# The norm behind the expert stage in place and tile by tile, GpSimd's steps on VectorE, and the order of a feed-forward's first weights

## The chip, the core and the metric

One core of a Trainium2 chip runs the whole program in one launch. Its engines work beside each other, each through its own queue in order: TensorE (PE: matrix products and transposes, with PEld for its weight loads), VectorE (DVE), ScalarE (ACT), GpSimd (POOL), and SyncE (SP), which here issues the DMA transfers. The metric is the device time of one execution in microseconds (us), the median over runs.

## What is computed

256 tokens of 1024 features go through two blocks, one behind the other, all in 32-bit floats.

```python
# block 1, twice (l = 0, 1)
mix = concat(retention, sliding_window, latent_attention)(x @ w_in[l]) @ w_out[l]
x = layer_norm(DEEPNORM_ALPHA * x + mix, ln1_g[l], ln1_b[l])
ffn = grouped_moe(x, router_w, router_bias, exp_w_gate_up[l], exp_w_down[l])
x = layer_norm(DEEPNORM_ALPHA * x + ffn, ln2_g[l], ln2_b[l])
# block 2, twice
h = h + 0.5 * swiglu(rms_norm_2(h, ffn1_norm[l]), ffn1_w1[l], ffn1_w3[l], ffn1_w2[l])
h = h + token_mixer(rms_norm_2(h, mix_norm[l]), w_in[l], ...)
h = h + 0.5 * swiglu(rms_norm_2(h, ffn2_norm[l]), ffn2_w1[l], ffn2_w3[l], ffn2_w2[l])
# at the end
rms_norm_2(h, final_norm)
```

`layer_norm` subtracts the mean over the features, divides by the deviation, multiplies by g and adds b. `rms_norm_2` divides by the root of the mean square and multiplies by a gain. `swiglu(u, w1, w3, w2)` is `(silu(u @ w1) * (u @ w3)) @ w2` with 2816 inner columns. `grouped_moe` has 16 experts, of which each token uses two.

## The kernel before

**Weights.** Every matrix product is made from two halves of each operand: a rounded high half and a low half, the rest. The weights stream in one fixed order from memory through six raw buffers (`raw`, DMA issued by SP); for each piece of up to 1024 columns ACT casts the high half (`whi`, L350) and DVE subtracts to the low one (`wlo`, L351), into five buffers each. A product is then three matmuls (helper `mm`, L411), two with `whi` and one with `wlo`; where the operand's halves lie side by side, the two with `whi` are one matmul of 512 columns (`gemm_halves`).

**Order.** The kernel is written as Python that issues instructions; a scheduler sets each engine's order from that. `tc.issue_after(x)` adds the condition that what follows on the engine of x stands behind x. `tc.manual_schedule(engines=...)` keeps the written order on the engines named (only the changed kernel uses it here).

**The expert stage and its norm.** `moe` ends with 60 filler matmuls (`keep_clock(WARM[2])`, tile `idle`), while DVE adds the stage's sum `ya` to the scaled input (L1197, tile `r`, four steps of 512 columns). `ln_hat` then takes statistics (L570, L571), the inverse root (`rsqrt`, eight small steps for each of the two token tiles of 128, L480 to L489) and writes the normalized `xh`, half by ACT (L583) and half by DVE (L584). Behind layer 0, `affine_T` transposes `xh` on PE (`trx`, L597) and applies g and b to the transposed blocks while it splits them (L605 to L607, tile `x2hl`): that is the input of the next attention, whose first products are `oq` (by `gemm_wide("cq")`) and `okv`. Beside it POOL makes the untransposed input `x` from `xh` and the broadcast rows `gb` (L1528, L1529). Behind layer 1, `xh` is transposed at L1538, DVE applies g and b (L1541, tile `h`, eight blocks), and `take_block` splits each block with the next gain and squares it (`xT_h`, L516, L517, and `sq`, L521).

**A feed-forward** (`ffn`, called four times; the last one has `then=None`) runs over f = 0 to 21, 128 inner columns each: u = x @ w1, v = x @ w3, then the down products f, which stand two steps later. The rms scale is not applied to the input but to u and v. It is computed at f = 0: `rms_columns` adds the squares up on DVE (L526), PE sums over the partitions (`rrow<-cperm,sq`, the column sums), DVE makes the mean (`ms`, L530) and the inverse root (`rsqrt_n`, ten small steps, L462 to L471, last `rs`) and puts it on a diagonal (`dg`, L535); PE turns that into a row (`rrow<-dg`, the row product, `rms_row`), ACT copies it (`row`, L542). Then DVE multiplies u by it (`fhp<-row,fhp`, L1324), ACT takes silu, DVE forms the product with v (L1327 to L1330), and ACT and DVE split it (`fhh`, L1331, L1332). u's low part is brought over by ACT (L1322) and added by DVE (`fhp<-u`, L1323); v's in the same way (`fvl`, L1328, and `fhp<-v`, L1329), and v's bank is free behind that. The last feed-forward also transposes the running state in its second step (`trh`, L1313, copied by ACT to `htok`, L1314).

**Elsewhere**, POOL makes the first product of the rotary step (`rope`, L651, 1024 columns in the attention and 1280 in the mixer), the gated norm weight of the retention (`gg`, L836) and, in the mixer, the sum of a pair of halves (`msum`, L1472, eight each).

## Time and profile before

| | |
|---|---|
| median of three runs | 1735.04 us (1733.93 to 1735.08) |
| profiled execution | 1737.42 us |
| its span | 1735.6 us |
| PE busy | 1673.4 us (96%) |
| DVE busy | 1278.7 us (74%) |
| ACT busy | 988.0 us (57%) |
| POOL busy | 56.2 us (3%) |

The profile is of one execution. Busy times are sums over the instructions of an engine; the idle time of an engine that is not the bottleneck costs nothing. Of interest is where PE idles, what it waits for there, and at which granted clock it works: in the rows below, PEclk is a share of full speed, 1.00 for 2.4 GHz and 0.50 for 1.2 GHz.

### The profile page before, as it was taken

What the parts mean: (1) busy time and instruction counts of PE and PEld (TensorE: products, weight loads), DVE (VectorE), ACT (ScalarE), POOL (GpSimd) and SP (SyncE); (2) the same over time, 40 slices, a digit from 0 to 9 for tenths busy, and PEclk for the clock granted to TensorE, in tenths of its full rate; (3) what the DMA queues carried; (4) which work ended last, traced back from release to release, by engine and by line L of the source; (5) the groups of instructions that cost most, each with busy time, mean ns of one, the idle gap of its engine ahead of it and who ended that gap; (6) DMA issues with size and microseconds to landing.
All of it is one profiled execution on the core that took longest, in us unless ns stands there. A gap on an engine that the chain in (4) does not pass through costs nothing.

```text
span 1735.6 us, 26627 instructions
## 1 busy us (share of the span) xinstructions
PE 1673.4 (96%) x10190; PEld 1458.9 (84%) x10190; DVE 1278.7 (74%) x2318; ACT 988.0 (57%) x1647; POOL 56.2 (3%) x52
## 2 busy tenths in 40 slices
PE   8998999899999989999999999999999999999997
PEld 8877777797777778999989989998999998988886
DVE  5768999876789987666865676667666775676666
ACT  5645777574577764455565544555555565465553
POOL 0001000200100000000000000000000000100000
PEclk9998999999899999999999999999999999999999
DMA  9432999553279864555533455554455452545540
GB/s 380 148 108 96 344 333 352 188 179 122 74 275 342 329 249 150 191 191 174 184 121 130 170 179 185 194 179 162 174 191 190 148 186 89 193 170 194 191 149 25
DMA packets 49141, 330.93 MB, mean 191 GB/s; under 512 B 5616, under 2 KB 5872, under 8 KB 13424
## 3 DMA queue, kind: packets, MB, share of 16 engines
q1 hardware_dynamic: 47664, 324.68, 51.6%
q10 hardware_dynamic: 1344, 4.49, 0.9%
q8 instruction: 82, 1.34, 0.3%
q14 instruction: 51, 0.42, 0.1%
HBM read 325.74 MB, written 1.05 MB: 188 GB/s over the span
## 4 chain that ended last, share of the span: by engine, by line
PE 67%; DVE 3%; ACT 1%; issue 1%; ACTq 0%; DVEq 0%
PE v L411 14%; PE f L411 14%; PE u L411 14%; PE ogt L411 6%; PE ogu L411 4%; PE oz L411 3%; PE obr L411 3%; PE yg L411 2%; PE ovp L411 2%; PE oq L411 2%; DVE wlo L351 1%; ACT whi L350 1%; PE sc L411 1%; PE po L411 1%; PE opl L411 1%
## 5 line engine op out<-in xcount | busy, mean ns | idle before, releaser
L351 DVE TENSOR_TENSOR wlo<-raw,whi 128x1024 fp32r<-128x1024 f32 (+2 forms) x611 | 736.4, 1212 | 319.0 <-ACT whi L350 303.5
L350 ACT CAST whi<-raw 128x1024 fp32r<-128x1024 f32 (+2 forms) x611 | 629.8, 1034 | 541.1 <-PE v L411 122.6
L411 PE MATMUL f<-fhh,whi 128*128 128x256 f32 x1056 | 196.5, 286 | 1.6 <-DVE fhh L1332 1.6
L411 PE MATMUL v<-xT_hf,whi 128*128 128x512 f32 x528 | 190.7, 399 | 5.4 <-DVE fhp L1329 5.4
L411 PE MATMUL u<-xT_hf,whi 128*128 128x512 f32 x528 | 189.3, 397 | 0.7 <-ACT htok L1314 0.7
L411 PEld LDWEIGHTS f<-fhh,whi 128*128 128x128 f32 x1056 | 166.4, 193 | 6.2 <-DVE fhh L1332 2.3
L411 PE MATMUL f<-fhh,wlo 128*128 128x256 f32 x528 | 149.9, 286 | 0.0
L411 PE MATMUL v<-xT_hf,wlo 128*128 128x256 f32 x528 | 148.5, 281 | 0.0
L411 PE MATMUL u<-xT_hf,wlo 128*128 128x256 f32 x528 | 148.3, 281 | 0.0
L411 PEld LDWEIGHTS v<-xT_hf,whi 128*128 128x128 f32 x528 | 99.7, 189 | 29.7 <-ACT fsl L1325 6.2
L411 PEld LDWEIGHTS u<-xT_hf,whi 128*128 128x128 f32 x528 | 99.1, 188 | 22.8 <-ACT htok L1314 0.9
L411 PE MATMUL ogu<-wlo,xgh 128*128 128x512 f32 x256 | 101.7, 397 | 4.3 <-DVE wlo L351 4.3
L411 PE MATMUL ogu<-whi,xgh 128*128 128x512 f32 x256 | 102.2, 399 | 0.1
L411 PEld LDWEIGHTS f<-fhh,wlo 128*128 128x128 f32 x528 | 101.3, 192 | 0.0
L411 PEld LDWEIGHTS u<-xT_hf,wlo 128*128 128x128 f32 x528 | 99.8, 189 | 1.0
L411 PEld LDWEIGHTS v<-xT_hf,wlo 128*128 128x128 f32 x528 | 100.3, 190 | 0.3
L411 PE MATMUL ogu<-whi,xgl 128*128 128x512 f32 x256 | 100.4, 392 | 0.0
L411 PE MATMUL ogt<-xT_hmx,whi 128*128 128x256 f32 x512 | 97.5, 287 | 0.0
L411 PE MATMUL yg<-whi,hh 128*128 128x512 f32 x256 | 84.6, 391 | 3.4 <-ACT hh L495 3.3
L411 PEld LDWEIGHTS ogt<-xT_hmx,whi 128*128 128x128 f32 x512 | 80.4, 191 | 3.0 <-issue 1.5
L411 PE MATMUL ogt<-xT_hmx,wlo 128*128 128x256 f32 x256 | 73.2, 287 | 0.0
L411 PE MATMUL v<-xT_h,whi 128*128 128x512 f32 x176 | 64.3, 403 | 2.7 <-DVE fhp L1329 2.7
(505 smaller groups left out, 3287.8 us busy)
## 6 DMA issues: line engine op xcount, KB each, us to landing
raw<-in_wflat_dram SPq DMA_DIRECT2D x276, 1024.0 KB, 4.8
raw<-in_wflat_dram SPq DMA_DIRECT2D x10, 960.0 KB, 4.7
raw<-in_wflat_dram SPq DMA_DIRECT2D x4, 992.0 KB, 4.8
gb<-in_rows_dram SPq DMA_DIRECT2D x6, 512.0 KB, 4.7
raw<-in_wflat_dram SPq DMA_DIRECT2D x4, 512.0 KB, 3.2
raw<-in_wflat_dram SPq DMA_DIRECT2D x2, 1008.0 KB, 6.1
raw<-in_wflat_dram SPq DMA_DIRECT2D x2, 976.0 KB, 6.8
raw<-in_wflat_dram SPq DMA_DIRECT2D x4, 384.0 KB, 6.1
```

The source lines that it names most:

```text
L350: nc.scalar.copy(hi[:, :n], r[:, c : c + n])
L351: self.split = nc.vector.tensor_tensor(out=lo[:, :n], in0=r[:, c : c + n], in1=hi[:, :n].bitcast(F32), op=ALU.subtract)
L411: return TE.matmul(out, lhsT=lhsT, rhs=rhs, start=start, stop=stop, skip_group_check=shared)
```

## The change

Five things are changed.

1. The norm behind the expert stage is made inside `moe`, in the place of the stage's input (`r`, which is x). Behind layer 0 the whole of tile 0 is written first (sum, statistics, inverse root by `rsqrt_n`, g and b by two DVE products for each half, transposes, split), then tile 1; g and b come from broadcast rows `gb2`, loaded early in `moe`, and POOL has no part in it. Behind layer 1 both tiles' inverse roots are made together. DVE's order is written out in both.
2. `gemm_wide("cq")` of layer 1 makes all of tile 0's products first, then tile 1's (`tail=8`).
3. The first product of `rope`, `gg` and `msum` are on DVE.
4. In `ffn`, the weights w1 of f = 1 and w2 of f = 0 and 1 stand behind the last `dg` on DVE.
5. Pools and helpers that are no longer needed (`ln2w`, `affine_T` behind layer 0, tiles `r2`, `xh`, `x2`) go.

```diff
--- before.py
+++ after.py
...
@@ -520,6 +520,8 @@
         )
         S.activation(out=squares[:, d], in_=hT[:, d], func=AF.Square)
 
+    rms_last = None
+
     def rms_columns(squares, work, o):
 
         for n in (4, 2, 1):
@@ -531,8 +533,9 @@
         rs = work.tile([P, 2], F32, name="rs2", tag="rs2", bufs=2)
         rsqrt_n(m, rs, 2, D**0.5)
         dg = work.tile([P, 2, P], F32, name="dg", tag="dg", bufs=1)
-        for t in range(2):
-            V.tensor_scalar(out=dg[:, t], in0=ident, scalar1=rs[:, t : t + 1], scalar2=None, op0=ALU.mult)
+        nonlocal rms_last
+        for t in range(2):
+            rms_last = V.tensor_scalar(out=dg[:, t], in0=ident, scalar1=rs[:, t : t + 1], scalar2=None, op0=ALU.mult)
         return rs, dg
 
     def rms_row(dg, work, o):
@@ -648,7 +651,7 @@
     def rope(src, swapped, dst, cosT, sinT):
 
         shape = [P, src.shape[1], T]
-        G.tensor_tensor(out=dst, in0=src, in1=cosT.unsqueeze(1).to_broadcast(shape), op=ALU.mult)
+        V.tensor_tensor(out=dst, in0=src, in1=cosT.unsqueeze(1).to_broadcast(shape), op=ALU.mult)
         V.tensor_tensor(out=swapped, in0=swapped, in1=sinT.unsqueeze(1).to_broadcast(shape), op=ALU.mult)
         return V.tensor_tensor(out=dst, in0=dst, in1=swapped, op=ALU.add)
 
@@ -672,7 +675,7 @@
...
         oq = [bank("acc", f"oq{t}") for t in range(2)]
-        gemm_wide("cq", hl, 8, [[(oq[t][:, :384], 0, 384)] for t in range(2)])
+        gemm_wide("cq", hl, 8, [[(oq[t][:, :384], 0, 384)] for t in range(2)], tail=8 if l else 1)
...
@@ -833,7 +836,7 @@
             th = work.tile([P, 256], F32, name="th", tag="rp1", bufs=2)
             S.activation(out=th, in_=og[t][:, :256], func=AF.Tanh, scale=0.5)
             V.scalar_tensor_tensor(out=th, in0=th, scalar=1.0, in1=og[t][:, :256], op0=ALU.add, op1=ALU.mult)
-            G.tensor_tensor(out=gg[:, t, :], in0=th, in1=rep("gn", l), op=ALU.mult)
+            V.tensor_tensor(out=gg[:, t, :], in0=th, in1=rep("gn", l), op=ALU.mult)
...
@@ -1024,6 +1027,12 @@
                 nc.sync.dma_start(
                     out=gb[:, j, :], in_=ap["rows"][base + j * D : base + (j + 1) * D].partition_broadcast(P)
                 )
+            gb2 = work.tile([P, 2, D], F32, name="gb2")
+            if l + 1 < NL:
+                for j in range(2):
+                    nc.sync.dma_start(
+                        out=gb2[:, j, :], in_=ap["rows"][base + (2 + j) * D : base + (3 + j) * D].partition_broadcast(P)
+                    )
...
@@ -1190,15 +1199,80 @@
                     with tc.issue_after(W.split.ins):
                         V.tensor_tensor(out=r[:, t, :], in0=r[:, t, :], in1=gb[:, j, :], op=op)
             keep_clock(WARM[2])
-            r2 = tok.tile([P, 2, D], F32, name="r2", tag="tok")
-            for t in range(2):
-                for n in range(2):
-                    c = slice(n * 512, (n + 1) * 512)
-                    V.scalar_tensor_tensor(
-                        out=r2[:, t, c], in0=r[:, t, c], scalar=ALPHA, in1=acc[t][n], op0=ALU.mult, op1=ALU.add
-                    )
...
-        return r2
+
...
+            def raw2(t, n):
+                c = slice(n * 512, (n + 1) * 512)
+                V.scalar_tensor_tensor(
+                    out=r[:, t, c], in0=r[:, t, c], scalar=ALPHA, in1=acc[t][n], op0=ALU.mult, op1=ALU.add
+                )
+                V.bn_stats(out=st2[:, t, n, :], in_=r[:, t, c])
+
+            def scale2(t0, t1):
+                for t in range(t0, t1):
+                    V.bn_aggr(out=mv2[:, t], in_=st2[:, t])
+                c = slice(t0, t1)
+                V.tensor_scalar(out=ve2[:, c], in0=mv2[:, c, 1], scalar1=LN_EPS, scalar2=None, op0=ALU.add)
+                rsqrt_n(ve2[:, c], rs2[:, c], t1 - t0, 1.0)
+
+            if l + 1 == NL:
+                with tc.manual_schedule(engines={V.engine}):
+                    for t in range(2):
+                        for n in range(2):
+                            raw2(t, n)
+                    scale2(0, 2)
+                    V.scalar_tensor_tensor(out=nb2, in0=mv2[:, :, 0], scalar=-1.0, in1=rs2, op0=ALU.mult, op1=ALU.mult)
+                    for t in range(2):
+                        S.activation(
+                            out=r[:, t, :512], in_=r[:, t, :512], func=AF.Identity, scale=rs2[:, t : t + 1],
+                            bias=nb2[:, t : t + 1],
+                        )
+                        V.tensor_scalar(
+                            out=r[:, t, 512:], in0=r[:, t, 512:], scalar1=mv2[:, t, 0:1], scalar2=rs2[:, t : t + 1],
+                            op0=ALU.subtract, op1=ALU.mult,
+                        )
+                return r, None
+            hl = new_hl("x2hl")
+
+            def whole(t, n):
+                c = slice(n * 512, (n + 1) * 512)
+                V.scalar_tensor_tensor(
+                    out=r[:, t, c], in0=r[:, t, c], scalar=mv2[:, t, 0:1], in1=gb2[:, 0, c], op0=ALU.subtract, op1=ALU.mult
+                )
+                V.scalar_tensor_tensor(
+                    out=r[:, t, c], in0=r[:, t, c], scalar=rs2[:, t : t + 1], in1=gb2[:, 1, c], op0=ALU.mult, op1=ALU.add
+                )
+                tr = bank("tr", "trx")
+                for j in range(4):
+                    TE.transpose(tr[:, j * P : (j + 1) * P], r[:, t, n * 512 + j * P : n * 512 + (j + 1) * P], ident)
+                return tr
+
+            def split2(t, n, tr):
+                o = (slice(None), slice(4 * n, 4 * n + 4), slice(t * P, (t + 1) * P))
+                split_evac(hl.high[o], hl.low[o], tr.rearrange("p (k s) -> p k s", k=4))
+
+            with tc.manual_schedule(engines={V.engine}):
+                raw2(0, 0)
+                raw2(0, 1)
+                scale2(0, 1)
+                a = whole(0, 0)
+                b = whole(0, 1)
+                split2(0, 0, a)
+                raw2(1, 0)
+                split2(0, 1, b)
+                raw2(1, 1)
+                scale2(1, 2)
+                a = whole(1, 0)
+                b = whole(1, 1)
+                split2(1, 0, a)
+                split2(1, 1, b)
...
+        return r, hl
 
     def overflow(l, xs, gates, G1, slot, acc, first, work):
 
@@ -1295,7 +1369,8 @@
         rs = row = h = None
         for f in range(NF):
             u, v = bank("mm", "u"), bank("tr", "v")
-            last = gemm_halves(f"f{i}w1", hl, 8, u)
+            with tc.issue_after(rms_last.ins) if f == 1 else nullcontext():
+                last = gemm_halves(f"f{i}w1", hl, 8, u)
             if f == 0:
                 with tc.issue_after(last.ins):
                     rs, dg = rms_columns(squares, work, ro)
@@ -1303,7 +1378,11 @@
             if f == 0:
                 with tc.issue_after(last.ins):
                     row = rms_row(dg, work, ro)
-            w2 = W.next(f"f{i}w2")
+            if f < 2:
+                with tc.issue_after(rms_last.ins):
+                    w2 = W.next(f"f{i}w2")
+            else:
+                w2 = W.next(f"f{i}w2")
             if f == 1 and not then:
                 h = tok.tile([P, 2, D], F32, name="htok", tag="tok")
                 for t in range(2):
@@ -1469,7 +1548,7 @@
             mg = work.tile([P, 512], F32, name="mg", tag="w2k", bufs=2)
             V.scalar_tensor_tensor(out=mg, in0=gts.pop(m), scalar=1.0, in1=o, op0=ALU.add, op1=ALU.mult)
             ms = work.tile([P, T], F32, name="msum", tag="w1k", bufs=2)
-            G.tensor_tensor(out=ms, in0=mg[:, :T], in1=mg[:, T:], op=ALU.add)
+            V.tensor_tensor(out=ms, in0=mg[:, :T], in1=mg[:, T:], op=ALU.add)
             split_evac(ml[0][:, m, :], ml[1][:, m, :], ms, 0.5)
 
         for m in range(8 + GATES_AHEAD):
@@ -1512,22 +1591,7 @@
         with tc.tile_pool(name="at1", bufs=1) as work:
             cb = work.tile([P, ap["cb1"].shape[1]], F32, name="cb1")
             residual, router = attention1(l, x, hl, work, cb)
-        r2 = moe(l, residual, router)
-        xh = ln_hat(r2, "ln2")
-        if l + 1 == NL:
-            break
-        with tc.tile_pool(name="ln2w", bufs=1) as work:
-            hl = new_hl("x2hl")
-            affine_T(xh, hl, col("ln2_g", l), col("ln2_b", l), work)
-            gb = work.tile([P, 2, D], F32, name="gb2")
-            base = (4 * l + 2) * D
-            for j in range(2):
-                nc.sync.dma_start(out=gb[:, j, :], in_=ap["rows"][base + j * D : base + (j + 1) * D].partition_broadcast(P))
-            x = tok.tile([P, 2, D], F32, name="x2", tag="tok")
-            for t in range(2):
-                G.tensor_tensor(out=x[:, t, :], in0=xh[:, t, :], in1=gb[:, 0, :], op=ALU.mult)
-                G.tensor_tensor(out=x[:, t, :], in0=x[:, t, :], in1=gb[:, 1, :], op=ALU.add)
...
+        x, hl = moe(l, residual, router)
     with tc.tile_pool(name="b2", bufs=1) as work:
         state = new_state("h0", work)
         for k2 in range(KT // 2):
@@ -1535,7 +1599,7 @@
             for j in range(2):
                 kt = 2 * k2 + j
                 for t in range(2):
-                    TE.transpose(tr[:, j * T + t * P : j * T + (t + 1) * P], xh[:, t, kt * P : (kt + 1) * P], ident)
+                    TE.transpose(tr[:, j * T + t * P : j * T + (t + 1) * P], x[:, t, kt * P : (kt + 1) * P], ident)
             for j in range(2):
                 kt = 2 * k2 + j
                 V.tensor_scalar(
```

Three places show how this moves instructions.

VectorE at the second feed-forward's start, from the end of the sums of squares (`sq`) to the scale's diagonal (`dg`). Before:

```order
L526 TENSOR_TENSOR sq<-sq 128x256
L351 TENSOR_TENSOR wlo<-raw,whi 128x1024
L530 TENSOR_SCALAR ms_10680<-rrow 128x2
L351 TENSOR_TENSOR wlo<-raw,whi 128x1024
L462 TENSOR_SCALAR rvi<-ms_10680 128x2
L351 TENSOR_TENSOR wlo<-raw,whi 128x1024
L463 TENSOR_SCALAR rvy<-rvi 128x2
L351 TENSOR_TENSOR wlo<-raw,whi 128x1024
L464 TENSOR_TENSOR rva<-rvy 128x2
L465 TENSOR_TENSOR rva<-rva,ms_10680 128x2
L466 SCALAR_TENSOR_TENSOR rvb<-rva,rvy 128x2
L351 TENSOR_TENSOR wlo<-raw,whi 128x1024
```

Now, to the end of the inverse root:

```order
L528 TENSOR_TENSOR sq<-sq 128x256
L532 TENSOR_SCALAR ms_10634<-rrow 128x2
L462 TENSOR_SCALAR rvi<-ms_10634 128x2
L463 TENSOR_SCALAR rvy<-rvi 128x2
L464 TENSOR_TENSOR rva<-rvy 128x2
L465 TENSOR_TENSOR rva<-rva,ms_10634 128x2
L466 SCALAR_TENSOR_TENSOR rvb<-rva,rvy 128x2
L467 TENSOR_TENSOR rva<-rvb 128x2
L468 TENSOR_TENSOR rva<-rva,ms_10634 128x2
L469 SCALAR_TENSOR_TENSOR rvy<-rva 128x2
L470 SCALAR_TENSOR_TENSOR rvy<-rvy,rvb 128x2
L471 TENSOR_SCALAR rs_10636<-rvy 128x2
```

And what follows there now:

```order
L538 TENSOR_SCALAR dg<-cperm,rs_10636 128x128 x2
L351 TENSOR_TENSOR wlo<-raw,whi 128x1024
L1403 TENSOR_TENSOR fhp<-row,fhp 128x256
L351 TENSOR_TENSOR wlo<-raw,whi 128x1024 x2
L1406 TENSOR_TENSOR fsl<-fsl,row 128x256
```

The weight splits (`wlo`) that stood between the small steps of the inverse root now stand behind `dg`; the first one behind it is f = 0's w2, and those of f = 1's w1 and w3 stand behind `fhp<-row`.

TensorE at the same start, around the row product (`rrow<-dg`), where u and v are the products with w1 and w3. Before, it is u of f = 2 that stands ahead:

```order
L411 MATMUL u<-xT_hf_10540,whi 128x512
L411 MATMUL u<-xT_hf_10540,wlo 128x256
L411 MATMUL rrow<-dg,cperm 128x256
L411 MATMUL v<-xT_hf_10540,whi 128x512
L411 MATMUL v<-xT_hf_10540,wlo 128x256
```

Now the column sums (`rrow<-cperm,sq`) and the row product stand close to each other:

```order
L411 MATMUL v<-xT_hf_10494,whi 128x512
L411 MATMUL rrow<-cperm,sq 128x2 x2
L411 MATMUL v<-xT_hf_10494,wlo 128x256
L411 MATMUL u<-xT_hf_10494,whi 128x512
L411 MATMUL v<-xT_hf_10494,whi 128x512
L411 MATMUL u<-xT_hf_10494,whi 128x512
L411 MATMUL rrow<-dg,cperm 128x256
L411 MATMUL u<-xT_hf_10494,wlo 128x256
L411 MATMUL u<-xT_hf_10494,whi 128x512
```

The u rows around the row product are of f = 1, whose two steps with `whi` stand ahead and whose first with `wlo` stands behind it; u and v of f = 1 and u of f = 2 stood between the two rrow rows before.

VectorE at the norm between the attention layers, from the first tile's statistics. Before, the inverse roots of the two tiles (`ln20` and `ln21`) stand woven into each other:

```order
L571 BN_AGGR mv_ln_3443<-st_ln_3442 128x2
L570 BN_STATS st_ln_3466<-r_3435 128x6
L573 TENSOR_SCALAR ve_ln_3447<-mv_ln_3443 128x1
L351 TENSOR_TENSOR wlo<-raw,whi 128x960
L480 TENSOR_SCALAR ln20i<-ve_ln_3447 128x1
L571 BN_AGGR mv_ln_3467<-st_ln_3466 128x2
L481 TENSOR_SCALAR ln20y<-ln20i 128x1
L573 TENSOR_SCALAR ve_ln_3471<-mv_ln_3467 128x1
L484 SCALAR_TENSOR_TENSOR ln20a<-ln20y,ve_ln_3447 128x1
L480 TENSOR_SCALAR ln21i<-ve_ln_3471 128x1
```

Now, from the end of the first tile's inverse root (`rs2l`; x_133 is the state, `ya` the experts' sum):

```order
L471 TENSOR_SCALAR rs2l<-rvy 128x1
L1244 SCALAR_TENSOR_TENSOR x_133<-x_133,mv_3438,gb_1465 128x512
L1247 SCALAR_TENSOR_TENSOR x_133<-x_133,rs2l,gb_1465 128x512
L1244 SCALAR_TENSOR_TENSOR x_133<-x_133,mv_3438,gb_1465 128x512
L1247 SCALAR_TENSOR_TENSOR x_133<-x_133,rs2l,gb_1465 128x512
L496 TENSOR_TENSOR x2hl<-trx,x2hl 128x4x128
L1211 SCALAR_TENSOR_TENSOR x_133<-x_133,ya_1803 128x512
L1214 BN_STATS st_3442<-x_133 128x6
L496 TENSOR_TENSOR x2hl<-trx,x2hl 128x4x128
L1211 SCALAR_TENSOR_TENSOR x_133<-x_133,ya_1804 128x512
L1214 BN_STATS st_3442<-x_133 128x6
```

Tile 0's four products with g and b and its first split now stand ahead of tile 1's sum and statistics.

## Rows read from the trace of the kernel before

**Rows 1.** PE's waits: tile <- what it waited for: us, times, longest us

```profile
PE v L411 <- DVE fhp L1329: 8.1, 3, 3.1
...
PE rrow L411 <- DVE dg L535: 2.6, 4, 0.9
...
PE trh L1313 <- ACT htok L1314: 1.8, 2, 1.1
...
PE trr L875 <- DVE ro L871: 1.5, 2, 0.7
```

**Rows 2.** timeline, second attention's norm: start, us, engine, operation [idle before <-releaser]

```profile
312.85 2.58 DVE L1197 SCALAR_TENSOR_TENSOR r<-x,ya 128x512 f32<-128x512 f32 x4
...
321.70 0.44 PE L597 MATMUL trx<-cperm,xh_ln 128*128 128x128 f32 x2 [1.62 <-ACT xh_ln L583]
...
322.69 4.92 POOL L1528 TENSOR_TENSOR x<-xh_ln,gb 128x1024 f32<-128x1024 f32 x2 [175.35 <-ACT xh_ln L583]
...
326.18 4.22 DVE L607 TENSOR_TENSOR x2hl<-aff,x2hl 128x256 fp32r<-128x256 f32 x2
...
330.46 0.44 PE L411 MATMUL oq<-whi,x2hl 128*128 128x384 f32 x1 [1.41 <-DVE x2hl L607]
```

**Rows 3.** windows: us, busy by engine (PE first), PEclk, DMA share, GB/s

```profile
324.20:327.60 3.40, 3.40 (x14) 3.31 (x13) 3.37 (x5) 1.14 (x3) 3.40 (x3) 0.50 0.09 36
...
665.60:669.00 3.40, 3.23 (x12) 2.97 (x13) 2.72 (x8) 1.75 (x5) 0.00 (x0) 0.50 0.66 280
...
1010.30:1017.10 6.80, 6.30 (x27) 6.00 (x28) 4.75 (x13) 2.81 (x8) 0.00 (x0) 0.50 0.31 130
...
1204.90:1211.70 6.80, 5.33 (x22) 5.08 (x23) 4.80 (x13) 2.66 (x7) 0.00 (x0) 0.50 0.44 154
```

**Rows 4.** timeline, first feed-forward's start

```profile
642.87 1.45 DVE L1541 TENSOR_SCALAR h<-trx,cols 128x256 f32<-128x256 f32 x3 [1.45 <-PE trx L1538]
...
644.76 0.79 PE L411 MATMUL u<-xT_h,whi 128*128 128x512 f32 x1
...
654.75 0.61 PE L411 MATMUL rrow<-cperm,sq 128*128 128x2 f32 x4
...
662.39 0.70 PE L411 MATMUL rrow<-dg,cperm 128*128 128x256 f32 x2 [0.57 <-DVE dg L535]
...
665.77 0.76 PE L411 MATMUL v<-xT_h,whi 128*128 128x512 f32 x1 [2.68 <-DVE fhp L1329]
```

**Rows 5.** timeline, second feed-forward's start

```profile
998.77 0.50 PE L411 MATMUL rrow<-cperm,sq 128*128 128x2 f32 x4
...
999.61 0.15 DVE L530 TENSOR_SCALAR ms<-rrow 128x2 f32<-128x2 f32 x1
...
999.68 1.22 DVE L351 TENSOR_TENSOR wlo<-raw,whi 128x1024 fp32r<-128x1024 f32 x1
...
1003.50 0.39 PE L411 MATMUL u<-xT_hf,whi 128*128 128x512 f32 x1
...
1003.85 0.39 PE L411 MATMUL u<-xT_hf,whi 128*128 128x512 f32 x1
...
1006.49 0.48 DVE L535 TENSOR_SCALAR dg<-cperm,rs 128x128 f32<-128x128 f32 x2
...
1007.02 0.70 PE L411 MATMUL rrow<-dg,cperm 128*128 128x256 f32 x2 [0.93 <-DVE dg L535]
...
1008.23 0.42 DVE L1324 TENSOR_TENSOR fhp<-row,fhp 128x256 f32<-128x256 f32 x1
```

**Rows 6.** timeline, third feed-forward's start

```profile
1203.31 0.70 PE L411 MATMUL rrow<-dg,cperm 128*128 128x256 f32 x2 [0.89 <-DVE dg L535]
```

**Rows 7.** timeline, VectorE, the chain in the first mixer

```profile
852.91 0.16 DVE L462 TENSOR_SCALAR rvi<-ms 128x2 int32<-128x2 int32 x1
...
854.89 0.48 DVE L535 TENSOR_SCALAR dg<-cperm,rs 128x128 f32<-128x128 f32 x2
```

**Rows 8.** groups on POOL: operation xcount | busy us, mean ns | idle before

```profile
L1472 POOL TENSOR_TENSOR msum<-mg 128x256 f32<-128x256 f32 x16 | 12.8, 800 | 207.1 <-DVE mg L1470 207.1
```

More of the change, by code (lines that the diff above doesn't have):

```diff
@@ L2 @@
 from collections import namedtuple
-from contextlib import ExitStack
+from contextlib import ExitStack, nullcontext
 import numpy as np
@@ L1192, in moe @@
             keep_clock(WARM[2])
-            r2 = tok.tile([P, 2, D], F32, name="r2", tag="tok")
-            for t in range(2):
-                for n in range(2):
-                    c = slice(n * 512, (n + 1) * 512)
-                    V.scalar_tensor_tensor(
-                        out=r2[:, t, c], in0=r[:, t, c], scalar=ALPHA, in1=acc[t][n], op0=ALU.mult, op1=ALU.add
-                    )
-            tap(f"r2_{l}", r2)
-        return r2
+            mv2 = work.tile([P, 2, 2], F32, name="mv2")
@@ new lines, in moe @@
+            ve2 = work.tile([P, 2], F32, name="ve2")
+            rs2 = work.tile([P, 2], F32, name="rs2l")
+            nb2 = work.tile([P, 2], F32, name="nb2")
+            st2 = work.tile([P, 2, 2, 6], F32, name="st2")
+            def raw2(t, n):
[4 more added lines that the diff above has]
+                V.bn_stats(out=st2[:, t, n, :], in_=r[:, t, c])
@@ L1203, in overflow @@
+            tap(f"x2_{l}", r)
+        return r, hl
     def overflow(l, xs, gates, G1, slot, acc, first, work):
@@ L1514, in build @@
             residual, router = attention1(l, x, hl, work, cb)
-        r2 = moe(l, residual, router)
-        xh = ln_hat(r2, "ln2")
-        if l + 1 == NL:
-            break
-        with tc.tile_pool(name="ln2w", bufs=1) as work:
-            hl = new_hl("x2hl")
-            affine_T(xh, hl, col("ln2_g", l), col("ln2_b", l), work)
-            gb = work.tile([P, 2, D], F32, name="gb2")
-            base = (4 * l + 2) * D
-            for j in range(2):
-                nc.sync.dma_start(out=gb[:, j, :], in_=ap["rows"][base + j * D : base + (j + 1) * D].partition_broadcast(P))
-            x = tok.tile([P, 2, D], F32, name="x2", tag="tok")
-            for t in range(2):
-                G.tensor_tensor(out=x[:, t, :], in0=xh[:, t, :], in1=gb[:, 0, :], op=ALU.mult)
-                G.tensor_tensor(out=x[:, t, :], in0=x[:, t, :], in1=gb[:, 1, :], op=ALU.add)
-            tap(f"x2_{l}", x)
+        x, hl = moe(l, residual, router)
     with tc.tile_pool(name="b2", bufs=1) as work:
```

## Prediction

> **What bounds the kernel now.** TensorE (PE) runs through nearly the whole span, so a change is worth what it does to PE's idle time and to the clock at which PE works. I read the list of PE's waits first, then the timeline around the places that the change touches, then the granted clock over the stretches behind their gaps. The waits at the start of a feed-forward are the largest that the change can reach: v behind fhp, rrow behind dg, and, in the last feed-forward, trh behind htok [rows 1]. The other place is the norm between the first and the second attention layer: PE idles 1.62 us before its first transposes (it has only filler matmuls before that) and 1.41 us in the middle of oq [rows 2]. Behind each gap stands a stretch at a granted clock of 0.50, the 1.2 GHz level [rows 3]. A fully busy stretch at that level does half its work, so it loses half of PE's busy time in it: 1.7 us behind the norm, 1.6, 3.15 and 2.7 in the first three feed-forwards. The last has none.
>
> So the four feed-forward starts now cost, idle plus clock: the first 0.57 + 2.68 + 1.6 = 4.9 [rows 3, 4], the second 0.93 + 3.1 + about 0.3 + 3.15 = 7.5 (3.1 is the longest of v's waits) [rows 1, 3, 5], the third 0.89 + 2.3 (what is left of v's 8.1) + 2.7 = 5.9 [rows 1, 3, 6], the last about 2.7 (trh 1.8, and some 0.9 around it) [rows 1]. Together 21 us. That is all that a better start can give back.
>
> **The feed-forward's chain: what is exposed.** Before, DVE spreads the chain over 999.61 (ms) to 1006.49 (dg) because weight splits of 1.22 us stand between its small steps [rows 5]. PE does not mind at first: between the column sums at 998.77 and the row product at 1007.02 it has the rest of u1, v1 and u2, so only 0.93 us of those 8.25 is idle. The change makes the chain short. From the uninterrupted chain in the mixer, rvi to dg takes 854.89 − 852.91 = 1.98 us [rows 7]. ms stands one step (0.2) ahead. dg to the row product is 0.53 and the columns to ms between 0.5 (their own time) and 0.84 [rows 5]; I take 0.6, since nothing stands in ms's way now. Columns to row product: 0.6 + 0.2 + 1.98 + 0.53 = 3.3 us instead of 8.25.
>
> But PE now has next to nothing to do in these 3.3 us. u1 needs the lower halves of f=1's w1, and their split stands behind dg on DVE. By the order, one matmul (first and third feed-forward) or four (second, fourth) stand between the columns and the row product. Pairs start 0.35 apart [rows 5], so that is about 0.3 or 0.75 us of work, beside 0.5 for the columns. **Gap one: 3.3 − 0.5 − 0.3 = 2.5, or 2.05 us.**
>
> Then the row product (0.70). On DVE the split of f=0's w2 comes first, beside the row product; fhp<-row follows 1.21 after the product's start, as before (1008.23 − 1007.02), and takes 0.35 to the next start; then w1's split, 1.22. So u1's first low matmul starts 1.21 + 0.35 + 1.22 + about 0.07 = 2.85 us after the row product, of which 0.70 is busy. **Gap two: 2.15 us.** What goes away in return is the wait of v for fhp, since u1 and v1, some 5.6 us, now stand between the row and the first down projection. Nothing hides the two gaps: all later PE work of this feed-forward stands behind u1.
>
> What the clock does: in the third feed-forward it fell by 1204.9, that is after 0.89 idle, 0.70 of row product and about 0.9 us of the next gap [rows 3, 6]. Two gaps above 2 us around the same 0.70 should do at least that. The fall cost 1.6 to 3.15 us [rows 3]; I take the middle, 2.4, for the first three, and 0.8 for the last, where the transposes break up the gaps.
>
> The Trainium skill (TensorE: Matmul & The Clock Gate, "What's actually happening") gives the throttled state as the one that follows wholly idle time; by that the row product between the gaps could keep the clock up, which is the first rival below. The trace speaks against it: the clock fell in the third feed-forward with that product in the middle.
>
> Sum by feed-forward, new cost minus old:
> first: 0.9 (columns, below) + 2.5 + 2.15 + 2.4 = 7.95, minus 4.9, plus 0.9 (late start, below): +3.9, bounds +1 to +6;
> second: 2.05 + 2.15 + 2.4 = 6.6, minus 7.5: −0.9, bounds −3 to +1;
> third: 2.5 + 2.15 + 2.4 = 7.05, minus 5.9: +1.1, bounds −1.5 to +2;
> last: 2.9 idle (gap two of 2.15 and about 0.75 left of gap one, as eight transposes now stand in it) + 0.8 − 2.7: +1.0, bounds −0.5 to +3.
> Together +5.1. The bounds are the ends of the clock's cost (nothing to 3.15) and, in gap one, 0.5 or 0.84 for columns to ms.
>
> **The first feed-forward's own part.** Of the norm ahead of it a weight split (1.22 us in rows 5) leaves the chain, which brings the transposes about 0.9 earlier, as some small steps come in its place. But DVE now does seven h before the first low half of xT_h, where three stood before. Three take 1.45 us [rows 4], so four more cost some 1.9. First u: 644.76 − 0.9 + 1.9, about 645.8, or 0.9 to 1.1 late. The low halves then come faster than before, so the lateness is the smaller end. The columns come later too: fhp<-u stands before the last two sums of squares, and it waits for the whole of u0. I put the columns at about the 654.75 of before [rows 4], with PE done with u0 and v0 some 0.9 us earlier, as no part of u1 is left to fill the time.
>
> **The norm between the attention layers.** Removed: a weight split inside the chain (about 1.2 us as in rows 5), the second tile's steps woven into the first's, four POOL products (two take 4.92 us [rows 2]), and DVE's trouble beside them: two x2hl subtractions took 4.22 us while POOL ran [rows 2]. Added on DVE: eight products of 512 columns at 0.645, as r (2.58 for four [rows 2]), half of them before the first transposes. The first tile: r and statistics 312.85 to some 315.5 with a split, chain 2.2, four products 2.6, so about 320.1; the first transposes are released about 319.3, the first oq about 322.1, 1.7 earlier than now. But tile 1's chain starts only behind it: about 2.4 for r and statistics, 1.2 for the two low halves, 2.3 for the chain, 1.3 for two products: transposes at about 327.5, oq at about 328.8. Tile 0's 24 oq matmuls are done at about 326, so PE idles some 3 us, and the clock may fall there as it does now (1.7). Before: 1.62 + 1.41 + some 1.5 of smaller waits + 1.7, about 6.2. After: 1.2 earlier transposes give that much, then 3 idle, 1.7 clock and about 0.5 of small waits: 5.2. **−1.0**, bounds −4 (tile 1 twice as fast in coming) and +1.5.
>
> **POOL's work on DVE.** Sixteen msum at 0.8 us mean on POOL [rows 8] become DVE steps of about 0.42, as fhp of the same size; rope and gg likewise. Of PE's waits only that of trr for ro, 1.5 us in two, comes behind one of them, gg [rows 1]. I cost them at nothing, since DVE is idle a quarter of the time and these stretches hold several us between producer and reader; where the cover were gone, eight msum would put 0.4 us each behind a mixer's end. Bounds −1.5 (ro) and +1.5. The broadcast rows load earlier in the expert stage and the three tables now stand ahead of a weight load at the second attention's start: I cost that at nothing, up to +2 for one load that comes late.
>
> **Sum:** +5.1 − 1.0 + 0 = +4.1. On the profiled execution's 1737.42 that is 1741.5; that execution lay 2.4 us above the median of 1735.04, so on the scale of the runs 1739.
>
> **Rivals.**
> The clock holds. If the row product between the gaps is enough to keep it at 2.4 GHz, the 8.0 us of clock in the new feed-forward costs vanish: 4.1 − 8.0 = −3.9, 1731. For it: the last feed-forward has about 2.7 us of broken gaps without a fall. Against: the third's fall.
> The gain comes whole. If the split of w1 is early enough that u1 runs on behind the row product, gap two (4 times 2.15) goes, and half of the clock's cost: 4.1 − 8.6 − 4 = −8.5, about 1726.5. For it: the halves by ACT are ready long before. Against: DVE's order puts two splits and fhp<-row ahead, and DVE runs in that order. So the change does what it says, by the order; this rival would need DVE to run far ahead of the rows.
> The clock stays down longer. If each start keeps it down for the long stretch, as in the second feed-forward (3.15), the last one too: 3 times 0.75 + 2.35 = +4.6, so 1743.5; with the norm's fall doubled, 1745.
>
> **How the numbers follow.** A difference under 0.2% (3.5 us) can't be told from none here. Forecast 0.50 (of it 0.30 above 1738.5, 0.20 within); clock holds 0.22 (half below 1731.6, half within); whole gain 0.10; longer low clock 0.18. Faster 0.21, same 0.31, slower 0.48. The range leaves out the whole gain and the far end of the long one: the terms' bounds together, not all at one end, give about −6.5 to +12, 1728.5 to 1747.
>
> **What would show it.** In the changed kernel: dg some 2.2 us behind ms with no split between; rrow waiting for dg about 2 us each time instead of 0.9; a new wait of u for wlo, four times some 2.1; v's wait for fhp gone; the first u about 645.8; a gap of about 3 us in oq before tile 1's transposes. Wrong would make it: u starting right behind the row product, no stretch at 0.50 behind the gaps, or the wait of v for fhp still there.

## The result, and the profile after

| | median, us | ratio to the kernel before, with its 95% interval |
|---|---|---|
| before | 1734.68 (1733.93 to 1735.08, 4 runs) | |
| changed | 1745.41 (1743.18 to 1747.37, 4 runs) | 1.0057 (1.0042 to 1.0073) |

The changed kernel is slower by 0.57%, or 7.3 to 12.7 us. The profiled execution is the slowest of its four, with a span of 1745.6 us; the one of before had 1735.6.

PE's waits in the changed kernel (engine, line, tile <- what it waited for: us in total, times, longest us):

```profile
PE u L411 <- DVE wlo L351: 6.5, 4, 2.1
PE rrow L411 <- DVE dg L538: 6.1, 4, 2.2
...
PE trx L1252 <- DVE x L1247: 4.1, 3, 2.9
PE oret L411 <- DVE sT L850: 2.9, 4, 1.1
...
PE rrow L411 <- DVE sq L528: 1.4, 2, 1.0
PE trh L1392 <- ACT htok L1393: 1.4, 2, 0.7
```

v's wait for fhp [rows 1] is no longer in the list; u's wait for wlo and a longer one of rrow for dg stand in its place. At the second feed-forward, in the timeline of the changed kernel (start us, us, engine, line, operation [idle before <-releaser]):

```profile
1006.86 0.50 PE L411 MATMUL rrow<-cperm,sq 128*128 128x2 f32 x4
1007.40 0.16 DVE L532 TENSOR_SCALAR ms<-rrow 128x2 f32<-128x2 f32 x1 [0.76 <-PE rrow L411]
...
1009.57 0.48 DVE L538 TENSOR_SCALAR dg<-cperm,rs 128x128 f32<-128x128 f32 x2
1009.97 1.22 DVE L351 TENSOR_TENSOR wlo<-raw,whi 128x1024 fp32r<-128x1024 f32 x1
1010.11 1.22 PE L411 MATMUL rrow<-dg,cperm 128*128 128x256 f32 x2 [1.40 <-DVE dg L538]
...
1011.77 0.42 DVE L1403 TENSOR_TENSOR fhp<-row,fhp 128x256 f32<-128x256 f32 x1 [0.58 <-ACT row L545]
1012.11 2.35 DVE L351 TENSOR_TENSOR wlo<-raw,whi 128x1024 fp32r<-128x1024 f32 x2
1013.39 0.58 PE L411 MATMUL u<-xT_hf,wlo 128*128 128x256 f32 x1 [2.06 <-DVE wlo L351]
```

Columns to row product take 3.25 us, where they took 8.25 [rows 5], and PE idles 1.40 and 2.06 us around the row product.

Where the time came in is seen from the start of the same instruction in both timelines. Each line is that start after minus before, so a step from one line to the next is what the stretch between them cost.

| instruction | before, us | after minus before |
|---|---|---|
| first oq of the second attention | 323.81 | −1.26 |
| its first trc (end of oq and okv) | 343.78 | −0.15 |
| its first oret (retention) | 407.82 | +0.55 |
| its first trr (end of the retention) | 426.46 | +4.88 |
| first u of the first feed-forward | 644.76 | +6.09 |
| column sums of the first mixer | 850.55 | +9.77 |
| column sums of the second mixer | 1392.09 | +10.74 |
| end of the last f | 1723.84 | +10.26 |

The second and third feed-forwards together cost 1.0 us, the last gives 0.5 back. Two stretches carry most: the retention (+4.3), which I had costed at nothing, and the first feed-forward (+3.7 behind its late first u, where I had 3.0: the 3.9 of the sum less the 0.9 of the late start).

In the retention, the kernel before, and then the changed one:

```profile
407.04 2.43 POOL L836 TENSOR_TENSOR gg<-th,reps 128x256 f32<-128x256 f32 x2 [5.51 <-DVE th L835]
407.21 0.55 DVE L847 TENSOR_TENSOR sT<-scr,cb 128x384 f32<-128x384 f32 x1
407.82 0.88 PE L411 MATMUL oret<-vv,sT 128*128 128x64 f32 x6 [0.48 <-DVE sT L847]
```

```profile
407.09 0.75 DVE L839 TENSOR_TENSOR gg<-th,reps 128x256 f32<-128x256 f32 x2
407.76 0.55 DVE L850 TENSOR_TENSOR sT<-scr,cb 128x384 f32<-128x384 f32 x1
408.37 0.88 PE L411 MATMUL oret<-vv,sT 128*128 128x64 f32 x6 [1.15 <-DVE sT L850]
```

gg on VectorE stands ahead of sT and PE waits 0.67 us longer. What follows up to the first trr is mostly clock. In the windows of the changed kernel (us, busy by engine, PE first, then PEclk):

```profile
409.60:423.20 13.60, 12.98 (x44) 10.24 (x42) 5.71 (x23) 0.00 (x0) 0.00 (x0) 0.51 0.22 77
661.90:672.10 10.20, 6.59 (x19) 5.20 (x20) 8.73 (x17) 1.68 (x4) 0.00 (x0) 0.50 0.41 129
1010.30:1017.10 6.80, 4.74 (x14) 3.54 (x15) 6.22 (x9) 2.07 (x3) 0.00 (x0) 0.52 0.38 133
1204.90:1215.10 10.20, 7.04 (x21) 5.54 (x22) 8.38 (x15) 2.13 (x4) 0.00 (x0) 0.51 0.43 141
```

The first line is the retention: half clock over 13.6 us. The others are the starts of the first three feed-forwards. Before, the retention had half clock for one short stretch:

```profile
412.60:416.00 3.40, 3.40 (x13) 2.91 (x14) 0.98 (x2) 0.00 (x0) 0.00 (x0) 0.56 0.14 58
```

By half of PE's busy time, as the prediction counts it, the retention lost some 1.7 us to the clock before and 6.5 now.

### The profile page after: what moved, and what is told of

Same layout as the page of the kernel before. It is cut to its first block, busy times and chain, and to the rows that moved or that the text cites. A ratio compares the mean times of both kernels' runs of the same rounds, so it can differ in the third digit from the quotient of the medians.

```text
span 1745.6 us, 26558 instructions
## 1 busy us (share of the span) xinstructions
PE 1678.8 (96%) x10190; PEld 1462.4 (84%) x10190; DVE 1282.8 (73%) x2330; ACT 981.7 (56%) x1641; POOL 18.2 (1%) x24
## 4 chain that ended last, share of the span: by engine, by line
PE 60%; DVE 2%; ACT 1%; issue 0%; ACTq 0%
PE u L411 15%; PE v L411 14%; PE f L411 14%; PE ogt L411 6%; PE oz L411 3%; PE obr L411 3%; PE ovp L411 2%; PE oq L411 2%; PE sc L411 1%; PE po L411 1%; PE opl L411 1%; PE rrow L411 0%; PE pt L1507 0%; DVE wlo L351 0%; ACT whi L350 0%
## 5 line engine op out<-in xcount | busy, mean ns | idle before, releaser
L411 PE MATMUL f<-fhh,whi 128*128 128x256 f32 x1056 | 192.1, 282 | 1.1 <-DVE fhh L1411 1.1
L411 PE MATMUL u<-xT_hf,whi 128*128 128x512 f32 x528 | 192.9, 403 | 0.2
L411 PEld LDWEIGHTS f<-fhh,whi 128*128 128x128 f32 x1056 | 162.2, 188 | 5.1 <-DVE fhh L1411 1.5
L411 PE MATMUL u<-xT_h,whi 128*128 128x512 f32 x176 | 66.6, 415 | 1.1 <-DVE xT_h L517 1.0
```

The costliest lines, as they stand in the source:

```text
L411: return TE.matmul(out, lhsT=lhsT, rhs=rhs, start=start, stop=stop, skip_group_check=shared)
```

## Experiments

Each ratio is to the kernel before on the same chip, in brackets its 95% interval; us are the ratio times 1735.

**The parts alone.** The feed-forward's two conditions alone:

```diff
 # before.py, with rms_last set in rms_columns
+            with tc.issue_after(rms_last.ins) if f == 1 else nullcontext():
                 last = gemm_halves(f"f{i}w1", hl, 8, u)
...
+            if f < 2:
+                with tc.issue_after(rms_last.ins):
+                    w2 = W.next(f"f{i}w2")
```

> The kernel before with only the two conditions in the feed-forward. Theory A: all four starts get the two gaps, about 2.2 and 2.1 us each, and lose v's wait; sum +5 to +6 us, 1740 to 1741. Rival B: no change or faster (1735 or less), since the shorter chain pays for the gaps and the clock holds.

Measured: 1.0004 (0.9994 to 1.0014), +0.7 us. Both gaps are there as in the changed kernel, and yet the time hardly moves:

```profile
PE u L411 <- DVE wlo L351: 6.5, 4, 2.1
PE rrow L411 <- DVE dg L538: 5.6, 4, 2.2
...
PE trh L1321 <- ACT htok L1322: 1.4, 2, 0.8
...
PE rrow L411 <- DVE sq L528: 0.7, 2, 0.4
```

Together 14.2 us, where the kernel before has 8.1 + 2.6 + 1.8 [rows 1] and 0.7 of u for htok, 13.2:

```profile
PE u L411 <- ACT htok L1314: 0.7, 1, 0.7
```

Theory A, by which the order was the main cost, fell here. (The profile is of one of the faster executions, 1733.58 us.)

The norms alone:

```diff
 # the changed kernel, without the two conditions, and
-        V.tensor_tensor(out=dst, in0=src, in1=cosT..., op=ALU.mult)      # rope; gg and msum likewise
+        G.tensor_tensor(out=dst, in0=src, in1=cosT..., op=ALU.mult)
```

> The kernel before with only the norm behind the expert stage in place, tile by tile (with the two cq passes), POOL keeping rope, gg and msum, the feed-forwards as before. What is to be told apart: the feed-forward's order alone costs 1.1 us, the changed kernel without it still 8. Theory C: half of that is the norm: at layer 0 the 2.9 us wait for tile 1's transposes with a clock fall eats the earlier start (0 to +1), at layer 1 the first u is 1.5 to 2.5 us later behind the expert stage; 1737.5 to 1740. Theory D: the norm is neutral as predicted (1733 to 1736) and all of the rest is the POOL steps.

Measured: 1.0035 (1.0023 to 1.0047), +6 us. Theory C, but more of it than expected. The steps from POOL alone (the kernel before with rope, gg and msum on VectorE):

> The kernel before with only rope's first product, gg and msum on VectorE. Theory C: gg ahead of sT makes PE wait 1.15 instead of 0.48 us for oret in the second attention, the clock falls there for about 10 us, +3 to +4 us: 1738.5 to 1740. Theory D: +7 to +8, 1743, if the norm is neutral. My prediction's own: 0 (1734 to 1737).

```diff
 # the kernel before
-        G.tensor_tensor(out=dst, in0=src, in1=cosT..., op=ALU.mult)      # rope; gg and msum likewise
+        V.tensor_tensor(out=dst, in0=src, in1=cosT..., op=ALU.mult)
```

Measured: 1.0036 (1.0021 to 1.0051), +6 us, with PE's wait for oret at 1.15 and the first trr at +4.15. That is more than theory C had, and theory D's ground is gone, as the norms cost 6 us too. The three parts alone sum to +13 (0.7 + 6 + 6), with intervals of some 2 us each; all together make 9.9 (7.3 to 12.7). The gap is within those intervals; the parts needn't add, as shown below for two gains.

**What of it can be taken back.** The changed kernel without the two conditions:

```diff
-            with tc.issue_after(rms_last.ins) if f == 1 else nullcontext():
-                last = gemm_halves(f"f{i}w1", hl, 8, u)
+            last = gemm_halves(f"f{i}w1", hl, 8, u)
...
-            if f < 2:
-                with tc.issue_after(rms_last.ins):
-                    w2 = W.next(f"f{i}w2")
```

> The changed kernel without the two conditions in the feed-forward (weights of f=0 and f=1 free again). Theory A: the two gaps at each feed-forward's start go (rrow for dg 6.1 us in four, u for wlo 6.5 us in four), v's wait for fhp (8.1 us) comes back, and the four starts cost what they did before: 5 to 6 us less than the changed kernel, about 1739.5 to 1740. Rival B: the starts are not what costs, the norm is: 1745.

Measured: 1.0041 (1.0027 to 1.0055), +7, and 2.8 us below the changed kernel by the ratios, with intervals that overlap. It is nearer to rival B: the order is a small part. The changed kernel with gg alone back on POOL:

```diff
-            V.tensor_tensor(out=gg[:, t, :], in0=th, in1=rep("gn", l), op=ALU.mult)
+            G.tensor_tensor(out=gg[:, t, :], in0=th, in1=rep("gn", l), op=ALU.mult)
```

> The changed kernel with only gg (two products of 256 columns per attention layer) back on POOL. Theory A: in the second attention, gg on VectorE stands ahead of sT, PE waits 1.15 us instead of 0.48 for oret, and the clock falls there for some 13 us; without it the end of the retention (first trr) comes back from +4.9 us to about 0 against the kernel before, and the kernel is 3 to 5 us faster than the changed one (about 1741). Rival B: the loss in the second attention comes from the in-place norm ahead of it (weights and tables late on SP); then nothing moves, 1745.

Measured: 1.0040 (1.0026 to 1.0055), 3 us below the changed kernel by the ratios, the low end of theory A, but their intervals overlap. In its profile, which is of the fastest of its five executions, the retention has no half clock (first trr at −1.68 against before). What gg costs was therefore asked again from the kernel before.

**gg's place.**

```diff
 # the kernel before with rope, gg and msum on VectorE
-            V.tensor_tensor(out=gg[:, t, :], in0=th, in1=rep("gn", l), op=ALU.mult)
+            ths.append(th)
...
+        with tc.issue_after(last_sT.ins):
+            for t in range(2):
+                V.tensor_tensor(out=gg[:, t, :], in0=ths[t], in1=rep("gn", l), op=ALU.mult)
```

> The kernel before with rope's first product, gg and msum on VectorE as in the run with these alone, but the two gg products stand behind the last sT on VectorE instead of ahead of the first. Theory C: what cost 7 us there is gg's place, 0.75 us ahead of sT; behind it, PE's wait for oret is 0.5 us again, the clock does not fall for long there, and the time is that of the kernel before: 1734.5 to 1736.5. Rival: VectorE's extra work as such (rope, msum, gg) costs: 1739 to 1743.

Measured: 0.9981 (0.9972 to 0.9990), so 3 us faster than before and 9.5 us faster than with gg ahead of sT. The work on VectorE is the same; its place decides. That it is faster than before, and than theory C had it, is not explained by the wait. The wait is back at its old length, and PE's windows behind it run at full clock:

```profile
408.52 0.88 PE L411 MATMUL oret<-vv,sT 128*128 128x64 f32 x6 [0.48 <-DVE sT L848]
```

```profile
412.00:415.00 3.00, 3.00 (x19) 2.31 (x18) 1.26 (x4) 0.00 (x0) 0.00 (x0) 1.00 0.55 232
```

Wait or clock? The next kernel keeps gg ahead of sT and fills PE's gaps with matmuls whose results nobody reads:

```diff
-            mm(sc[:, T : T + P], k[:, P:], q[:, P:], True, True)
+            m = mm(sc[:, T : T + P], k[:, P:], q[:, P:], True, True)
+            if l and h < 2:
+                with tc.issue_after(m.ins):
+                    keep_clock((9, 12)[h])
```

> The kernel before with rope, gg and msum on VectorE (gg ahead of sT), and 9 and 12 filler matmuls on PE, whose results are not used, in the gaps before the first and the second oret of the second attention. Theory C, with the clock as the larger part: the gaps stay, 0.7 us longer than before, but the granted clock stays at 1.00 in the scores behind them; first trr at +1 instead of +4 us against the kernel before; 1736 to 1738. Rival: the loss is waiting, not clock: 1741 to 1743.

Measured: 1.0019 (1.0010 to 1.0028), 3 us less than without the fillers by the ratios, with intervals that overlap. The windows of the kernel without fillers and of the one with them:

```profile
409.00:412.00 3.00, 2.36 (x13) 1.91 (x13) 1.02 (x2) 0.00 (x0) 0.00 (x0) 0.50 0.73 221
412.00:415.00 3.00, 3.00 (x11) 2.22 (x10) 0.00 (x0) 0.00 (x0) 0.00 (x0) 0.50 0.31 128
```

```profile
409.00:412.00 3.00, 3.00 (x26) 2.63 (x25) 1.07 (x2) 0.00 (x0) 0.00 (x0) 1.00 0.45 139
412.00:415.00 3.00, 2.57 (x21) 2.08 (x20) 1.02 (x2) 0.00 (x0) 0.00 (x0) 1.00 0.51 216
```

The clock holds, and the first trr stands at −0.77 instead of +4.15. So in this place, in these profiles, nearly all of the loss is clock. The rest of the way to the late gg (6.6 us by the ratios) stays open: the fillers also push a later score product back, and in this profile a half-clock stretch at the expert stage lasted 6.8 us (from 486 us), where the profile of the late gg had 3.4 (from 485 us).

**The norms.** The norm behind layer 1 alone in place, layer 0 as before:

```diff
 # the kernel before, in moe behind keep_clock(WARM[2])
+            if l + 1 == NL:
+                with tc.manual_schedule(engines={V.engine}):
+                    for t in range(2):
+                        for n in range(2):
+                            raw2(t, n)
+                    scale2(0, 2)
...
+                return r
             r2 = tok.tile([P, 2, D], F32, name="r2", tag="tok")
```

> The kernel before with the norm in place behind layer 1 alone (layer 0 as before, POOL and feed-forwards as before). Theory C: of the 5.9 us that both norms cost, some 3 us are the later first u (the chain 1 us longer, seven h ahead of the first low half 2 us): 1738 to 1739.5. If layer 0's norm costs the most: 1735 to 1737. If layer 1 carries all of it: 1740 to 1742.

Measured: 1.0021 (1.0011 to 1.0030), +3.6 us, as theory C has it. Its first u comes 2.9 us later behind the last ya. Its chain from the first sum to ACT's products is 9.0 us, with the weight split of 1.22 inside; the kernel before takes 8.1 with one too. First this kernel, then the kernel before:

```profile
629.03 0.69 DVE L1201 SCALAR_TENSOR_TENSOR x<-x,ya 128x512 f32<-128x512 f32 x1
629.64 1.22 DVE L351 TENSOR_TENSOR wlo<-raw,whi 128x1024 fp32r<-128x1024 f32 x1
...
638.07 1.52 ACT L1221 ACTIVATE x<-x,nb,rs2l 128x512 f32<-128x512 f32 x2 [9.57 <-DVE nb L1219]
```

```profile
631.96 2.59 DVE L1197 SCALAR_TENSOR_TENSOR r<-x,ya 128x512 f32<-128x512 f32 x4
...
640.09 0.81 ACT L583 ACTIVATE xh_ln<-r,nb_ln,ln20r 128x512 f32<-128x512 f32 x1 [8.66 <-DVE nb_ln L582]
```

For layer 0 some 2.5 us are left of the 6, less certain than either number, and what in it costs (the tiles in turn, the products on VectorE, the rows loaded earlier) was not run apart. There the profile of the changed kernel shows what was expected:

```profile
322.17 0.63 PE L1252 MATMUL trx<-cperm,x 128*128 128x128 f32 x4 [0.82 <-DVE x L1247]
322.55 0.42 PE L411 MATMUL oq<-whi,x2hl 128*128 128x384 f32 x1
...
329.87 0.63 PE L1252 MATMUL trx<-cperm,x 128*128 128x128 f32 x4 [2.91 <-DVE x L1247]
```

From the last ya of layer 0 to the first trc it gains 0.4 there and 0.5 with the norms alone, where half clock follows for 3.4 us. It loses 0.8 to 0.9 in the profiles of the kernels with gg on POOL and without the conditions, where it follows for 6.8. None of these edits is in that stretch, so the length of the clock's fall, and not the code, makes the difference there.

**The order that pays.** Only f = 1's w2 stands behind the chain; the splits of f = 0's w2 and f = 1's w1 and w3 stay ahead of it:

```diff
-            with tc.issue_after(rms_last.ins) if f == 1 else nullcontext():
-                last = gemm_halves(f"f{i}w1", hl, 8, u)
+            last = gemm_halves(f"f{i}w1", hl, 8, u)
...
-            if f < 2:
+            if f == 1:
                 with tc.issue_after(rms_last.ins):
                     w2 = W.next(f"f{i}w2")
```

In the changed kernel:

> The changed kernel, but only f=1's w2 stands behind the chain; f=0's w2 and f=1's w1 are free and get split ahead of it. Theory A: the chain is as short as in the changed kernel (about 3.3 us from the column sums to the row product) but u1 runs beside it, so both gaps shrink to well under 1 us in sum and the clock holds: 17 us of idle time less and some of the clock, 1725 to 1730. Rival B: the row product and u wait for something else (the chain itself): 1740 to 1745.

Measured: 0.9965 (0.9950 to 0.9979), 6 us faster than before and 16 faster than the changed kernel; the median, 1730.85, lies just above theory A's range. And in the kernel before, with nothing else changed:

> The kernel before with one condition: f=1's w2 stands behind the chain (dg); norm, POOL steps and all else as before. From the same condition in the changed kernel (13 us less than without any condition): if that gain is the feed-forwards' own, 1722 to 1726, faster than the kernel before; if it was owed to the changed norm ahead of the first feed-forward, 1730 to 1735.

Measured: 1721.80 us, 0.9926 (0.9907 to 0.9945), 13 us faster than before: the gain is the feed-forwards' own. The second feed-forward's start in it:

```profile
990.35 0.50 PE L411 MATMUL rrow<-cperm,sq 128*128 128x2 f32 x4
991.21 0.15 DVE L532 TENSOR_SCALAR ms<-rrow 128x2 f32<-128x2 f32 x1
...
994.27 0.59 PE L411 MATMUL rrow<-dg,cperm 128*128 128x256 f32 x2
...
996.19 0.39 PE L411 MATMUL u<-xT_hf,wlo 128*128 128x256 f32 x1 [0.62 <-DVE wlo L351]
...
999.55 0.47 PE L411 MATMUL v<-xT_hf,whi 128*128 128x512 f32 x1 [0.51 <-DVE fhp L1336]
```

```profile
992.00:996.00 4.00, 3.56 (x20) 2.86 (x19) 3.75 (x11) 2.13 (x3) 0.00 (x0) 1.00 0.31 117
996.00:1000.00 4.00, 3.30 (x18) 2.69 (x19) 3.83 (x7) 3.02 (x5) 0.00 (x0) 1.00 0.90 334
```

The chain is nearly as short as in the changed kernel (3.9 us from columns to row product, 3.25 there), but PE works on u1 and v1 beside it. No gap opens ahead of the row product; behind it u, now that of f = 2, waits 0.62 us here and 1.48 in the third feed-forward. v waits 0.51 instead of 3.1 us, and the clock stays at 1.00 through the second and third feed-forward. Which of the two freed weights matters more was not run apart; u's wait for `wlo` in the changed kernel points at f = 1's w1.

**Together.** The kernel before with this one condition, rope and msum on VectorE, and gg there behind the last sT (the diffs of the three runs named):

> The kernel before (norms as they were) with what paid in the runs apart: f=1's w2 behind the chain and nothing else held, rope and msum on VectorE, gg on VectorE behind the last sT. If the two gains add (13.4 and 3.7 us): 1718. If the second was owed to where the clock happened to fall: 1721 to 1722, that of the first alone.

Measured: 0.9921 (0.9906 to 0.9937), 1723.89 us. The gains do not add: it is where the one condition alone is. Its profile has gg behind sT, a wait for oret of 0.48, and still a half-clock stretch of 6.8 us in the retention, so the late gg doesn't always hold the clock, and the 3 us by which it beat the kernel before aren't shown to be its own. And the changed kernel with both flaws mended, by the same two diffs:

> The changed kernel with its two flaws mended (only f=1's w2 held behind the chain; gg behind the last sT), its norms left as they are. From the kernel with the first mended (1730.9), less what gg's place cost (3 to 7): 1724 to 1728. It tells what the two norms cost when nothing else is wrong: the distance to the run with the norms as before, expected 3 to 6 us.

Measured: 0.9937 (0.9924 to 0.9950), 1725.28 us, within what was expected. Against the kernel just above, the norms cost 0.0016, about 3 us; the intervals overlap, so this alone does not settle them.

## Why the prediction was right, and where it was not

The direction and the range held; the size was under half (+4 for +10). In the changed kernel's profile the miss of some 6 us lies nearly all in one place: from the first trc to the first trr of the second attention the table goes from −0.15 to +4.88, 5.0 us for which I had nothing. That the other terms come near their sum is in part luck, as shown below.

- **The chain and the two gaps, as mechanism: right.** Columns to row product 3.25 us (3.3 forecast), gap two 2.06 (2.15), gap one 2.21, 1.40 and 2.20 (2.5, 2.05, 2.5). v's wait went.
- **Their sum: right in the changed kernel, from terms that were not.** I had +5.1 for the starts, of which 0.9 was the norm's late u; the table's steps behind the first u sum to the +4.2 that is left. But the gaps were somewhat shorter than forecast; the last feed-forward idles about 2 us (the waits of trh, rrow and u), not 2.9, and has no fall of the clock, for which I had 0.8; and half clock cost some 3.3, 2.4 and 3.5 us in the first three (half of PE's 6.59, 4.74 and 7.04 in the windows above), not 2.4 each. On the kernel before, the condition alone costs only 0.7 (−1.0 to +2.4). One gain of it stood elsewhere in my sum and was priced too low: the condition takes a weight split out of the norm ahead of the first feed-forward. In the profile of the condition alone the first u comes 1.6 us earlier behind the last ya (0.9 forecast), and the half clock that stood behind that norm before is gone; the prediction, which lists four stretches, leaves that one out. The first line is the kernel before, the second the condition alone, whose own gaps then bring 6.8 us of half clock:

```profile
641.70:648.50 6.80, 6.03 (x23) 5.21 (x24) 5.63 (x13) 4.98 (x14) 0.00 (x0) 0.50 0.00 0
641.00:649.00 8.00, 6.77 (x35) 4.96 (x34) 7.22 (x20) 5.96 (x13) 0.00 (x0) 1.00 0.00 1
```

- **The first feed-forward's own part: too small.** The first u was forecast 1.0 late and is 1.65 late behind the last ya of layer 1 in the changed kernel, and layer 1's norm alone costs 3.6. The step that failed here is that a weight split leaves the chain and so brings the transposes 0.9 earlier: it left because of the condition on the weights, not because of the norm, and the chain without it is as long as the old one with it (8.0 us from the first sum at 636.51 to ACT's products at 644.53, against 8.1). The old chain without a split, in the profile of the condition alone, takes 7.0: sums and statistics in turns are 0.4 us longer, and the inverse root of both tiles, which now starts behind the last statistics, brings the other 0.6. The seven h ahead of the first low half stand there as forecast.
- **The norm between the attention layers: its places right, its sum not settled.** First oq 1.5 earlier counted from the last ya (1.7 forecast), a wait of 2.91 (3), a clock fall of 3.4 us (1.7 lost, as taken). The forecast's sum drops what is left of the first wait: 1.62 less 1.2, about 0.4, where PE waits 0.38 and 0.82 ahead of tile 0's transposes. Profiles give −0.5 to +0.9 (−1.0 forecast); the times leave room for more.
- **POOL's work at nothing: wrong, and the largest miss.** This is the step that failed. I looked at who waits for gg (ro), not at what queues behind it on VectorE. That is sT, behind 0.75 us of gg, with PE waiting for it. The bounds of −1.5 to +1.5 had no clock in them; the part alone costs 6 us (3.6 to 8.8), and the same work with gg behind the last sT none.
- **The rivals.** The clock did not hold; the whole gain did not come with the change's order, but came with the order that left f = 1's w1 free, nearly as that rival had it: w1's split is early, and u1 runs ahead of the row product. The longer low clock came, 10.2 us in the first and in the third feed-forward, but the largest of it in the retention.

## What to carry to other kernels

An ordering condition that clears a chain must leave the work that hides the chain ahead of it: hold back what is needed last, not all that is late. A step moved to a busier engine is priced by what stands behind it on its new queue and who waits for that, not by its own reader. Where half-clock stretches follow gaps, as they do here, a short new wait is to be priced with the stretch that can follow.

## What was not expected of the hardware

In the changed kernel's retention the clock stayed at half over 13.6 us in which PE was busy for 12.98; a busy PE by the profile's count did not bring it back sooner. In the 10 us ahead of that fall the profile lists one wait of PE, the 1.15 us for sT. Half-clock stretches also come in different places from one kernel's profile to the next where the code is the same: the retention with the late gg had none in one and 6.8 us in two others. All four profiles with gg ahead of sT and no fillers have between 6.8 and 13.7 us of it in the retention; of the ten others six have none, one 3.4 and three 6.8. One profile shows what a fall costs there; what it is worth over many executions only the timed runs show.
